# Two transformer blocks in one kernel: how the second block's gate tiles, pooling products and attention heads are joined

## The chip, the cores and the metric

The kernel runs on one core of a Trainium2 chip. The time is the device time of that core in microseconds (us), taken over several executions; the median is given. A profiled execution is one more execution, with its own time. Of the core's engines the text names TensorE (PE, matrix products), VectorE (DVE), ScalarE (ACT), GpSimd (POOL) and SyncE (SP, which here only issues DMAs).

## The reference

Everything is float32, batch 1, 512 tokens, width 2048. A first block of two layers (windowed attention, latent attention, gates) comes ahead; the change does not touch its arithmetic. The second block adds 16 meta tokens in front and computes, with `W_in` of 2048 x 12288 cut in eight:

```
h = rmsnorm_2(x, gain); zin = h @ w_in
q, k, v, g_attn, u, g_pool, m_attn, m_pool = split(zin)     # 1024 each, m_* 2048
o_attn = stick_breaking_attention(q, k, v) * silu(g_attn)   # 8 heads of 128
y_attn = o_attn @ w_attn_up
pooled = multiscale_pool(u)       # trailing means over 2, 4, 8, 16 tokens, less u
mixed  = einsum('blgc,gcd->blgd', pooled, pool_w)           # 4 groups of 256
o_pool = mixed * pool_scale * silu(g_pool)
y_pool = o_pool @ w_pool_up
merged = sigmoid(m_attn) * y_attn + sigmoid(m_pool) * y_pool
out = rmsnorm_2(x + merged @ w_out, final_gain)[:, 16:]
```

In stick-breaking attention a query takes sigmoid(z) of a key times the product of (1 - sigmoid(z)) over the keys between.

## The kernel before

**Products.** Activations lie with features on the 128 partitions and tokens along the columns. Every float32 operand is split into a high part (fp32r, cast by ACT) and a low part (difference, DVE), and a product is three matmuls (`mm3`, L167). A plain tile of 128 output features takes 2 weight blocks of 8 chunks, 48 matmuls of 512 columns; from an operand of 1024 features it takes one block and 24 matmuls. A weight block (512 KB) goes through `w_raw` (L192, SP's queue, three buffers), then `load_w_split` (L239) on ACT and DVE; `next_w` (L249) keeps two split blocks ready.

**Pairs.** Two tiles together can be made by a seven-product scheme (`run_pair`, L345): 168 matmuls of half the columns in place of 192 half-column ones. It needs sums of the activations, the eight t sets (`t_set`, L323: two POOL additions, four DVE sums, two splits each), and sums of weight blocks, which POOL's queue makes in DRAM ahead of time (`plan_sums`, `sum_step`, L204 and L218; 39 pairs, four DMAs each, paced by weight loads). The second block's pairs run with `tset`, which `t_build` (L1156) makes as a side task.

**Order.** PE's instructions run in the order in which the program writes them; the other engines' order is chosen when the kernel is built, close to the program's. `SEQ2` (L63) is the order of the second block's tiles: `gp` (silu gates of the pool, 8), then for each of four groups two `u` tiles and the pool product `pw`, then `k`, `q`, `v` (8 each), `ma`, `mp` (16 each), `ga` (8, plain), `pu` (pool-up, 16), `au` (attention-up, 16). `_plain` (L73) says which tiles are not made in pairs: `ga`, and `gp` below GPLAIN.

**Side tasks.** Beside the tiles run generators: `scales` (L879), `t_build`, eight `sb_head` (L989) and `meta_final` (L1101). `start_side` gives one a due time, `tick` (after each `mm3`) steps at most three of them whose time has come, and a `yield n` sets the next due time n later. The time is the kernel's own count: a matmul of 512 columns adds 512 / 2.4 + 3 = 216.3, in nanoseconds by intention. `need(ready)` (L307) runs the side tasks at once until a condition holds. The head with number n starts at the tile that `HEADS` (L43) gives, ahead of that tile's matmuls.

**A head** loads its q, k, v from DRAM, splits them, transposes v (`vt`), makes the scores (`zA`, `zB`, `zC`), softplus and suffix sums (`suf`, on POOL; split into `sufh`, `sufl`), the meta part (`zm`), a second phase on the same PSUM tiles (`zA<-sufl`), `rm`, then exp and the output (`so`). `meta_final` waits for all heads, and adds the meta tokens' part to each head's output (`om`), times the gate, into `oa`, which the `au` tiles read; a `need` stands ahead of the first `au` tile.

**Memory.** Working tiles come from one pool of 76 slots (`NSLOT`, L39). X2, the block's input, takes 32 of them until the last `ga` tile, the t sets 32 until the first `ga` tile, three tiles of scales stay. DMAs of the second block: `load` (L1151), the heads' loads and most stores are issued by POOL; weight loads by SP; the stores of the sigmoid gates by ACT. `o_load` (L1169) brings the eight `o_pool` tiles (`ol`) back for the pool-up tiles.

Of the kernel before, what the change touches and what calls it, by code (L numbers as in the profile page):

```python
# [18 lines left out]
P = 128  # L19
S = 512  # L20
# [17 lines left out]
GRP = 3  # L38
NSLOT = 76  # L39
M2 = NM // 2  # L40
GPLAIN = 4
EARLYT = 4
HEADS = {("ga", 0): 0, ("ga", 1): 1, ("ga", 3): 2, ("ga", 5): 3, ("ga", 6): 4, ("pu", 0): 5, ("pu", 3): 6, ("pu", 5): 7}  # L43
HN = S // 2
NPLAIN = 4
NSPILL = 8
SUMPAIRS = 39
NSIDE = 3
TP_WAIT = 4000

# [12 lines left out]
def _order2():  # L63
    seq = [("gp", i) for i in range(8)]
    for g in range(4):
        seq += [("u", 2 * g), ("u", 2 * g + 1), ("pw", g)]
    for kind, n in (("k", SB), ("q", SB), ("v", SB), ("ma", NC), ("mp", NC), ("ga", SB), ("pu", NC), ("au", NC)):
        seq += [(kind, i) for i in range(n)]
    return seq

# [33 lines left out]
def trunk_kernel(ctx, tc, xT, w_in, w_qkv, w_out, w_in2, w_pool, w_aup, w_pup, w_out2, metaT, vec, cst, outT):  # L104
# [41 lines left out]
    def split(src, name, cols=S, hi=None, lo=None):  # L146
        if hi is None:
            hi = slot(name + "h", F32R, cols)
            lo = slot(name + "l", F32R, cols)
        nc.scalar.copy(hi, src)  # L150
        tt(lo, src, f32(hi), ALU.subtract)
        return hi, lo
# [96 lines left out]
    def next_w():  # L249
        while len(wready) < 2 and wq:  # L250
            if callable(wq[0][0]):
                make, n = wq.popleft()
                load_w_split(make(), n)
            else:
                load_w_split(*load_w_dma())
            last_pe[1] += 1
            if last_pe[1] > 12 and last_pe[1] % 3 and presum:
                sum_step()
        return wready.popleft()

# [728 lines left out]
    def sb_head(hd):  # L989
        raw = {}  # L990
        for kind, n in (("k", W), ("q", S), ("v", W)):
            raw[kind] = slot(kind + "r", F32, n)
            nc.gpsimd.dma_start(raw[kind], qkvd[kind][:, hd, :])
        yield 6000
        kh, kl = split(raw["k"], "k", W)
        qh, ql = slot("qh", F32R), slot("ql", F32R)
        nc.scalar.mul(qh, raw["q"], SB_SCALE)
        stt(ql, raw["q"], SB_SCALE, f32(qh), ALU.mult, ALU.subtract)
        vf = raw["v"]
        nc.gpsimd.tensor_copy(halves(VM[:, hd * NM:(hd + 1) * NM]), halves(vf)[:, :, :M2])  # L1000
        raw = None
        yield 1500
        vh, vl = v_split(vf)
        yield 600
        zb = [ps_at("zA"), ps_at("zB"), ps_at("zC", 256)]

        def region(j, frm=None):
            frm = j if frm is None else frm
            bk, c0 = WHERE[j]
            return bk, slice(c0 + (frm - j) * P, c0 + (NB - j) * P)  # L1010

        def ks(j):
            return slice(token(j), token(j) + P)

        mm3(zb[0], kh[:, ks(0)], kl[:, ks(0)], qh, ql, True, False)
        mm(zb[0][:, :P], ident_r, maskB[:, :P], False, True)
        mm3(zb[2], kh[:, ks(2)], kl[:, ks(2)], qh[:, 256:], ql[:, 256:], True, False)
        mm(zb[2][:, :P], ident_r, maskB[:, :P], False, True)
        mm(zb[1], ident_r, maskB, True, False)
        mm3(zb[1][:, :384], kh[:, ks(1)], kl[:, ks(1)], qh[:, 128:], ql[:, 128:], False, False)  # L1020
        mm3(zb[1][:, 384:], kh[:, ks(3)], kl[:, ks(3)], qh[:, 384:], ql[:, 384:], False, True)
        spf = [softplus(z, "sp") for z in zb]
        spt = [split(t, "sp", t.shape[1]) for t in spf]

        suf = {}
        below = spf[1][:, 384:]
        for j in (2, 1, 0):
            n = (NB - j) * P
            bk, sl = region(j)
            t = slot("suf", F32, n)  # L1030
            nc.gpsimd.tensor_tensor(t[:, P:], spf[bk][:, sl][:, P:], below, ALU.add)
            nc.gpsimd.tensor_copy(t[:, :P], spf[bk][:, sl][:, :P])
            below = t
            suf[j] = split(t, "suf", n)
        suf[3] = tuple(t[:, 384:] for t in spt[1])
        yield 2500
        zo = (hd % 2) * 240 + 112
        nc.vector.tensor_copy(halves(zwh[:, zo:zo + NM]), halves(f32(kh))[:, :, :M2])
        nc.vector.tensor_copy(halves(zwl[:, zo:zo + NM]), halves(f32(kl))[:, :, :M2])
        win = slice(zo - NM * hd, zo - NM * hd + P)  # L1040
        pm = ps_at("zm")
        mm3(pm, zwh[:, win], zwl[:, win], qh, ql, True, True)
        if hd == 0:
            nc.scalar.copy(zM, pm)
        else:
            tt(zM, pm, zM, ALU.add)
        yield 6000

        def sp(j, frm=None):
            bk, sl = region(j, frm)  # L1050
            return spt[bk][0][:, sl], spt[bk][1][:, sl]

        for j in range(NB):
            bk, sl = region(j)
            mm2(zb[bk][:, sl], tri[:, :P], *sp(j), False, True)
            if j < NB - 1:
                n = (NB - 1 - j) * P
                bk, sl = region(j, j + 1)
                mm2(zb[bk][:, sl], none, suf[j + 1][0][:, :n], suf[j + 1][1][:, :n], False, True)
        yield 1000  # L1060
        pm = ps_at("rm")
        mm2(pm, nwin[:, 112 - NM * hd:240 - NM * hd], *suf[0], True, True)
        if hd == 0:
            nc.scalar.copy(RM, pm)
        else:
            tt(RM, pm, RM, ALU.add)
        At = []
        for z in zb:
            a = slot("A", F32, z.shape[1])
            act(a, z, AF.Exp)  # L1070
            At.append(split(a, "A", z.shape[1]))
        yield 7000
        o = ps_at("so")
        for j in (0, 1, 2, 3):
            bk, sl = region(j)
            vs = slice(j * P, (j + 1) * P)
            mm3(o[:, j * P:], vh[:, vs], vl[:, vs], At[bk][0][:, sl], At[bk][1][:, sl], j == 0, j == 3)
        orw = slot("oraw")
        nc.scalar.copy(orw, o)
        o_raw[hd] = orw  # L1080

    def token(j):

# [5 lines left out]
            transp(tp[:, j * P:(j + 1) * P], vf[:, token(j):token(j) + P])  # L1089
        return split(tp, "v")  # L1090

    o_raw = {}
    gates = {}
    oa = [None] * SB
    od = tc.dram_tile([P, 8, S], F32, name="od")
    gpd = tc.dram_tile([P, 8, S], F32, name="gpd")
    ypd = tc.dram_tile([P, NC, S], F32, name="ypd")
    sgd = tc.dram_tile([P, 2 * NC, S], F32, name="sgd")
    qkvd = {k: tc.dram_tile([P, SB, n], F32, name=k + "d") for k, n in (("k", W), ("q", S), ("v", W))}

    def meta_final():  # L1101
        while len(o_raw) < SB:
            yield 500
        sp = split(softplus(zM, "spm"), "spm")
        yield 4000
        pm = ps_at("lm")
        mm2(pm, tri[:, P:], *sp, True, True)
        L = slot("Lm")
        nc.gpsimd.tensor_tensor(L, zM, RM, ALU.add)
        tt(L, pm, L, ALU.add)  # L1110
        act(L, L, AF.Exp)
        Ah, Al = split(L, "Am")
        pv = ps_at("vmt", P)
        transp(pv, VM)
        vm = slot("vm", F32, P)
        nc.scalar.copy(vm, pv)
        vmh, vml = split(vm, "vm", P)
        yield 5000
        for hd in range(SB):
            mh = small.tile([P, 2 * P], F32R, tag="mh", name="mh", bufs=2)  # L1120
            nc.vector.tensor_scalar(mh[:, :P], f32(vmh), rowm[:, hd:hd + 1], None, op0=ALU.mult)
            nc.vector.tensor_scalar(mh[:, P:], f32(vml), rowm[:, hd:hd + 1], None, op0=ALU.mult)
            ps = ps_at("om")
            mm3(ps, mh[:, :P], mh[:, P:], Ah, Al, True, True)
            t = o_raw.pop(hd)
            tt(t, ps, t, ALU.add)
            tt(t, t, gates.pop(("a", hd)), ALU.mult)
            oa[hd] = split(t, f"oa{hd}")
            yield 3000

# [19 lines left out]

    def load(src, name, n=S):  # L1151
        t = slot(name, F32, n)
        nc.gpsimd.dma_start(t, src)
        return t

    def t_build(get, upto):  # L1156
        while len(tset) < upto:
            n = len(tset)
            tset.append(t_set(get(n), get(n + 8)))
            yield 5000  # L1160

    def u_order(t):

# [3 lines left out]
        return u  # L1167

    def o_load(c):  # L1169
        op[c] = split(load(od[:, c, :], "ol"), f"o{c}")  # L1170

    start_side(t_build(x2, 8))
    for kind, i in SEQ2:
        if (kind, i) in HEADS:
            if kind == "ga" and i == 0:
# [5 lines left out]
        if kind == "pw":  # L1181
            wh, wl = next_w()
            rhs = [pooled.pop(2 * i), pooled.pop(2 * i + 1)]
            for d in range(2):
# [4 lines left out]
                    mm3(ps, wh[:, sl], wl[:, sl], *rhs[k], k == 0, k == 1)  # L1189
                t = slot("mix")  # L1190
                stt(t, ps, vcol(V_PSC + 2 * i + d), gp, ALU.mult, ALU.mult)
                nc.gpsimd.dma_start(od[:, 2 * i + d, :], t)
        elif kind == "pu":
            gp = load(sgd[:, NC + i, :], "sgl")
            yp = slot("yp")
# [20 lines left out]
        elif kind == "ga":  # L1216
            if i == 0:
                tset = None
            gates["a", i] = gate_silu(run_gemm(2, 8, x2), sr, "ga")
            if i == SB - 1:  # L1220
                X2 = None
                for c in range(8):
# [216 lines left out]
```

## Time and profile before

| | us |
|---|---|
| median of 3 runs | 2771.2 |
| lowest and highest run | 2769.97, 2774.9 |
| the profiled execution | 2775.9 |
| its span, first to last instruction | 2774.1 |
| PE busy in it | 2648.2 |
| DVE busy | 1863.0 |
| ACT busy | 1318.2 |
| POOL busy | 640.4 |

The mean granted TensorE clock of the execution is 0.976 of full speed. The first gate tile of the second block starts at 1372.6 us of the span, the last pair of its input products ends at 2189.8, the pool-up tiles run from 2345 to 2486.7, the attention-up tiles follow, and the output products fill the rest. A profile line such as `pw<-pdh,wh` names what is written and read by the program's names.

### The profile page before, as it was taken

The page shows a single profiled execution, that of the slowest core. Times are in us where ns is not written, and L with a number is a line of the kernel's source. Part 1 is how long each engine was busy: PE and PEld are TensorE (multiplying, and loading weights), DVE is VectorE, ACT ScalarE, POOL GpSimd, SP SyncE. Part 2 cuts the span into 40 slices and gives each one's busy share as a digit, 9 for nine tenths or more (in the row PEclk, how much of TensorE's full clock was granted, in tenths as well). Part 3 has the DMA queues.
Part 4 walks back from the last instruction along what each step waited for, and adds up shares of the span by engine and source line. Part 5 has one row for each costly group of instructions (what it writes and reads, how often), then busy time and mean ns, then how long its engine had stood idle before and what let it go on. Part 6 is the DMA issues. An engine that isn't in the chain of part 4 may idle for free. (4 is left out here: it accounts for less than half of the span.)

```text
span 2774.1 us, 39556 instructions
## 1 busy us (share of the span) xinstructions
PE 2648.2 (95%) x15313; PEld 2314.3 (83%) x15313; DVE 1863.0 (67%) x2697; ACT 1318.2 (48%) x2170; POOL 640.4 (23%) x645
## 2 busy tenths in 40 slices
PE   8999999999999999999979789999999998899897
PEld 6888888888788888888758779999999876778697
DVE  7767667644477667665687657677777655666687
ACT  5445455522344455543345333436666666533353
POOL 4111122222111123234433210000000223324412
PEclk9999999999999999999989899999999999999999
DMA  5454544577554454567638445545555523355465
GB/s 176 121 138 121 136 120 121 165 210 204 149 132 124 128 130 125 132 167 217 186 105 245 124 127 159 158 153 158 159 161 159 176 77 107 113 157 171 124 188 182
DMA packets 129980, 416.64 MB, mean 150 GB/s; under 512 B 15344, under 2 KB 19824, under 8 KB 129792
## 3 DMA queue, kind: packets, MB, share of 16 engines
q1 hardware_dynamic: 90176, 283.15, 32.5%
q0 software_dynamic: 34864, 122.50, 18.5%
q10 hardware_dynamic: 4752, 8.46, 0.8%
q8 instruction: 120, 1.97, 0.3%
q14 instruction: 68, 0.56, 0.1%
HBM read 376.17 MB, written 119.67 MB: 179 GB/s over the span
## 5 line engine op out<-in xcount | busy, mean ns | idle before, releaser
L245 ACT CAST wh<-wr 128x1024 fp32r<-128x1024 f32 (+2 forms) x448 | 462.1, 1031 | 663.4 <-PE mm L159 349.8
L128 DVE TENSOR_TENSOR wl<-wr,wh 128x1024 fp32r<-128x1024 f32 (+2 forms) x448 | 580.0, 1298 | 237.2 <-ACT wh L245 223.1
L159 PE MATMUL mm<-hh,wh 128*128 128x512 f32 x1024 | 410.7, 401 | 7.0 <-ACT wh L245 6.8
L159 PE MATMUL mm<-hl,wh 128*128 128x512 f32 x1024 | 404.9, 395 | 2.9 <-DVE hl L131 2.9
L159 PE MATMUL mm<-hh,wl 128*128 128x512 f32 x1024 | 404.7, 395 | 2.7 <-DVE wl L128 2.7
L221 POOL DMA_DIRECT2D wsd<-in_w_in x136 | 95.7, 705 | 708.9 <-PE mm L159 502.8
L159 PEld LDWEIGHTS mm<-hh,wl 128*128 128x128 f32 x1024 | 193.3, 189 | 48.9 <-DVE wl L128 4.3
L159 PEld LDWEIGHTS mm<-hh,wh 128*128 128x128 f32 x1024 | 193.8, 189 | 42.9 <-ACT wh L245 6.8
L159 PEld LDWEIGHTS mm<-hl,wh 128*128 128x128 f32 x1024 | 193.8, 189 | 40.3 <-DVE hl L131 5.1
L245 ACT CAST wh<-ws 128x1024 fp32r<-128x1024 f32 x117 | 122.7, 1049 | 160.7 <-PE y L159 109.4
L159 PE MATMUL y<-t34h,wl 128*128 128x256 f32 (+1 forms) x624 | 176.3, 282 | 0.0
L159 PE MATMUL y<-t34l,wh 128*128 128x256 f32 (+1 forms) x624 | 175.6, 281 | 0.0
L159 PE MATMUL y<-t34h,wh 128*128 128x256 f32 (+1 forms) x624 | 175.6, 281 | 0.0
L128 DVE TENSOR_TENSOR wl<-ws,wh 128x1024 fp32r<-128x1024 f32 x117 | 143.0, 1223 | 28.5 <-ACT wh L245 26.1
L159 PE MATMUL x<-Xl,wh 128*128 128x256 f32 (+1 forms) x544 | 154.6, 284 | 0.0
L159 PE MATMUL x<-Xh,wl 128*128 128x256 f32 (+1 forms) x544 | 154.2, 284 | 0.0
L159 PE MATMUL x<-Xh,wh 128*128 128x256 f32 (+1 forms) x544 | 153.9, 283 | 0.0
L159 PEld LDWEIGHTS y<-t34h,wh 128*128 128x128 f32 x624 | 117.7, 189 | 0.0
L159 PEld LDWEIGHTS y<-t34l,wh 128*128 128x128 f32 x624 | 117.4, 188 | 0.0
L159 PEld LDWEIGHTS y<-t34h,wl 128*128 128x128 f32 x624 | 117.2, 188 | 0.0
L128 DVE TENSOR_TENSOR ws<-ws,wr 128x1024 f32<-128x1024 f32 x78 | 106.4, 1364 | 2.6
L159 PEld LDWEIGHTS x<-Xh,wh 128*128 128x128 f32 x544 | 103.4, 190 | 0.0
(1048 smaller groups left out, 7216.8 us busy)
## 6 DMA issues: line engine op xcount, KB each, us to landing
wr<-in_w_in SPq DMA_DIRECT2D x254, 512.0 KB, 3.7
wsd<-in_w_in POOLq DMA_DIRECT2D x136, 512.0 KB, 5.3
wr<-in_w_out SPq DMA_DIRECT2D x95, 512.0 KB, 4.4
ws<-wsd SPq DMA_DIRECT2D x39, 512.0 KB, 4.3
wr<-wsd SPq DMA_DIRECT2D x39, 512.0 KB, 4.1
wsd<-in_w_out POOLq DMA_DIRECT2D x20, 512.0 KB, 5.8
xd<-xn SPq DMA_DIRECT2D x32, 256.0 KB, 3.3
sgd<-sga ACTq DMA_DIRECT2D x32, 256.0 KB, 2.2
```

The lines of the kernel that those rows point to most:

```text
L128: nc.vector.tensor_tensor(out, a, b, op)
L159: last_pe[0] = nc.tensor.matmul(out, a, b, start=start, stop=stop, skip_group_check=True).ins
L221: i = nc.gpsimd.dma_start(dst, src, **kw)
L245: nc.scalar.copy(hi, raw)
```

## The change

Five things, all in the second block:

1. GPLAIN 4 to 6: gate tiles 4 and 5 are plain; one pair less, so 38 pairs of weight sums. The sums' pace goes from two in three weight loads to three in four. `t_build` starts 9000 later in the kernel's time, and leaves 7000 between sets instead of 5000 (also for the four sets that it makes in the output stage).
2. In each pooling group the two `k` tiles of the same number (one pair) stand between the `u` pair and `pw`.
3. Heads start at other tiles, and most of their yields are longer.
4. `load` and the heads' loads are issued by SP instead of POOL.
5. A head's output goes to DRAM (`od`, by ACT's queue), the attention gates go to DRAM (`gad`, by POOL's), and `meta_final` reads both back, two heads ahead (`o_gate`). The pool outputs get an array of their own (`opd`).

```diff
-GPLAIN = 4
+GPLAIN = 6
-HEADS = {("ga", 0): 0, ("ga", 1): 1, ("ga", 3): 2, ("ga", 5): 3, ("ga", 6): 4, ("pu", 0): 5, ("pu", 3): 6, ("pu", 5): 7}
+HEADS = {("ga", 0): 0, ("ga", 2): 1, ("ga", 4): 2, ("ga", 6): 3, ("pu", 1): 4, ("pu", 3): 5, ("pu", 5): 6, ("pu", 7): 7}
-SUMPAIRS = 39
+SUMPAIRS = 38
@@ _order2
-        seq += [("u", 2 * g), ("u", 2 * g + 1), ("pw", g)]
-    for kind, n in (("k", SB), ("q", SB), ("v", SB), ("ma", NC), ("mp", NC), ("ga", SB), ("pu", NC), ("au", NC)):
+        seq += [("u", 2 * g), ("u", 2 * g + 1), ("k", 2 * g), ("k", 2 * g + 1), ("pw", g)]
+    for kind, n in (("q", SB), ("v", SB), ("ma", NC), ("mp", NC), ("ga", SB), ("pu", NC), ("au", NC)):
@@ next_w
-            if last_pe[1] > 12 and last_pe[1] % 3 and presum:
+            if last_pe[1] > 12 and last_pe[1] % 4 and presum:
@@ sb_head
-            nc.gpsimd.dma_start(raw[kind], qkvd[kind][:, hd, :])
-        yield 6000
+            nc.sync.dma_start(raw[kind], qkvd[kind][:, hd, :])
+        yield 9000
...
-        yield 1500
+        yield 2000
         vh, vl = v_split(vf)
-        yield 600
+        yield 1000
...
-        yield 2500
+        yield 3500
...
-        yield 6000
+        yield 7000
...
-        o_raw[hd] = orw
+        nc.scalar.dma_start(od[:, hd, :], orw)
+        o_raw.append(hd)
@@ meta_final
+    def o_gate(hd):
+        return load(od[:, hd, :], "or"), load(gad[:, hd, :], "gar")
...
+        og = [o_gate(0), o_gate(1)]
...
-            t = o_raw.pop(hd)
+            t, g = og.pop(0)
+            if hd + 2 < SB:
+                og.append(o_gate(hd + 2))
             tt(t, ps, t, ALU.add)
-            tt(t, t, gates.pop(("a", hd)), ALU.mult)
+            tt(t, t, g, ALU.mult)
@@ load, t_build, o_load
-        nc.gpsimd.dma_start(t, src)
+        nc.sync.dma_start(t, src)
...
-            yield 5000
+            yield 7000
...
-        op[c] = split(load(od[:, c, :], "ol"), f"o{c}")
+        op[c] = split(load(opd[:, c, :], "ol"), f"o{c}")
...
-    start_side(t_build(x2, 8))
+    start_side(t_build(x2, 8), 9000)
...
-                nc.gpsimd.dma_start(od[:, 2 * i + d, :], t)
+                nc.gpsimd.dma_start(opd[:, 2 * i + d, :], t)
...
-            gates["a", i] = gate_silu(run_gemm(2, 8, x2), sr, "ga")
+            nc.gpsimd.dma_start(gad[:, i, :], gate_silu(run_gemm(2, 8, x2), sr, "ga"))
```

## Rows read from the trace of the kernel before

**Rows 1.** The page's first two parts: PE's busy time with its share of the span and its instructions, and the granted TensorE clock in forty equal slices, in tenths of full speed (9 is 0.9 or more).

```profile
PE 2648.2 (95%) x15313; PEld 2314.3 (83%) x15313; DVE 1863.0 (67%) x2697; ACT 1318.2 (48%) x2170; POOL 640.4 (23%) x645
...
PEclk9999999999999999999989899999999999999999
```

**Rows 2.** The list of PE's waits over the whole span: who waited on which tile and for whom, then us in total, how many times, and the longest.

```profile
PE pw L159 <- ACT pdh L150: 25.9, 7, 6.5
PE z L159 <- ACT t12h L150: 13.4, 3, 7.7
PE csum L159 <- ACT csh L150: 10.2, 2, 8.4
...
PE mm L159 <- DVE wl L128: 6.8, 3, 4.2
PE vt L163 <- DMA vr<-vd: 6.0, 1, 6.0
PE zA L159 <- DVE sufl L128: 5.7, 6, 1.4
PE pw L159 <- DVE pdl L128: 5.6, 4, 1.8
PE mm L159 <- ACT o0h L150: 4.7, 1, 4.7
...
PE zA L159 <- ACT qh L997: 3.2, 1, 3.2
...
PE vt L163 <- ACT RM L1064: 2.9, 1, 2.9
PE mm L159 <- ACT o1h L150: 2.3, 1, 2.3
```

**Rows 3.** The table of stretches. Each stretch begins and ends at the first matmul of a piece on PE's timeline (those of the pool products begin where the pair before has ended); its width in us, then the busy time of PE, its weight loads, DVE, ACT and POOL with counts, the granted clock, the busy share of the DMA engines and GB/s.

```profile
1372.60:1396.38 23.78, 15.27 (x56) 11.64 (x54) 19.23 (x26) 8.97 (x17) 10.75 (x7) 0.78 0.35 95
1396.38:1407.59 11.21, 11.21 (x50) 9.01 (x49) 9.15 (x12) 4.03 (x8) 6.33 (x6) 1.00 0.50 140
1430.01:1469.40 39.39, 23.96 (x169) 22.46 (x168) 32.40 (x40) 18.71 (x27) 16.20 (x15) 0.78 0.52 133
1469.40:1489.27 19.87, 19.87 (x170) 19.87 (x169) 16.43 (x19) 12.46 (x18) 8.13 (x9) 1.00 0.91 302
1489.27:1509.75 20.48, 20.48 (x170) 20.44 (x168) 15.30 (x19) 11.61 (x18) 8.57 (x9) 1.00 0.94 272
1509.75:1520.12 10.37, 5.62 (x14) 3.30 (x13) 7.67 (x9) 3.04 (x6) 3.07 (x4) 0.67 0.70 183
...
1610.40:1628.38 17.98, 6.48 (x15) 3.90 (x14) 7.48 (x9) 3.08 (x6) 11.19 (x11) 0.62 0.20 62
1628.38:2189.80 561.42, 561.42 (x4706) 561.42 (x4704) 420.88 (x504) 291.55 (x375) 17.95 (x32) 1.00 0.52 159
2189.80:2344.99 155.19, 138.38 (x636) 112.91 (x635) 91.43 (x131) 101.18 (x183) 48.62 (x62) 0.96 0.30 92
2344.99:2486.70 141.71, 128.95 (x562) 104.17 (x563) 88.15 (x140) 65.26 (x113) 44.64 (x71) 0.93 0.45 143
2486.70:2632.19 145.49, 136.76 (x577) 109.15 (x576) 96.74 (x111) 45.69 (x61) 67.83 (x67) 0.98 0.48 152
```

**Rows 4.** POOL's timeline in the gate stretch and at the last pooling group: start, duration, instruction, and in brackets the idle time before it and what ended it.

```profile
1414.91 1.38 POOL L439 TENSOR_TENSOR gpg<-gpg,gpa 128x512 f32<-128x512 f32 x1 [9.27 <-ACT gpa L135]
...
1417.22 1.34 POOL L330 TENSOR_TENSOR ra<-Xh,Xl 128x528 f32<-128x528 f32 x1
...
1617.74 1.25 POOL L1138 TENSOR_TENSOR pl<-uf 128x527 f32<-128x527 f32 x1 [2.13 <-ACT uf L1166]
```

**Rows 5.** DVE's timeline, the same columns, in the gate stretch, at the last pooling group and late in the attention-up tiles.

```profile
1381.39 1.54 DVE L128 TENSOR_TENSOR t<-ra,rb 128x264 f32<-128x264 f32 x1
...
1388.18 0.43 DVE L128 TENSOR_TENSOR t<-ra,rb 128x264 f32<-128x264 f32 x1
...
1390.89 0.68 DVE L128 TENSOR_TENSOR csl<-xgq,csh 128x512 fp32r<-128x512 f32 x1
...
1622.64 0.69 DVE L131 SCALAR_TENSOR_TENSOR pd<-pl,uf 128x512 f32<-128x512 f32 x1 [4.57 <-POOL pl L1138]
1624.07 0.69 DVE L128 TENSOR_TENSOR pdl<-pd,pdh 128x512 fp32r<-128x512 f32 x1 [0.74 <-ACT pdh L150]
...
2582.85 0.69 DVE L128 TENSOR_TENSOR ym<-mm,sgl 128x512 f32<-128x512 f32 x1 [2.89 <-DMA sgl<-sgd]
```

**Rows 6.** POOL's timeline, the same columns, at the start of the pool-up tiles and at the start of the last head.

```profile
2344.52 1.26 POOL L439 TENSOR_TENSOR gag<-gag,gaa 128x512 f32<-128x512 f32 x1 [9.89 <-ACT gaa L135]
2345.73 3.76 POOL L1153 DMA_DIRECT2D ol<-od  x7
...
2404.48 0.55 POOL L1197 DMA_DIRECT2D ypd<-yp  x1 [2.08 <-DVE yp L128]
2405.01 0.54 POOL L993 DMA_DIRECT2D kr<-kd  x1
```

**Rows 7.** The view of the tile om: durations in ns (lowest, median, highest), the first and the last start in us, and the shape. Each of the eight steps has two of these matmuls.

```profile
L159 PE MATMUL om<-Amh,mh x16: 392/395/468, 2450.4 to 2475.3; 128*128 128x512 f32 x16
```

**Rows 8.** The list of DMA issues: transfer, queue, count, size of each, and the median us from issue to landing.

```profile
ol<-od POOLq DMA_DIRECT2D x8, 256.0 KB, 4.6
```

**Rows 9.** The list of waits of SP's queue from 2180 to 2600 us, with the columns of rows 2.

```profile
SPq L193 <- DVE wl L128: 371.6, 52, 23.1
```

More of the change, by code (lines that the diff above doesn't have):

```diff
@@ L1090, in v_split @@
         return split(tp, "v")
-    o_raw = {}
-    gates = {}
+    o_raw = []
     oa = [None] * SB
     od = tc.dram_tile([P, 8, S], F32, name="od")
+    opd = tc.dram_tile([P, 8, S], F32, name="opd")
+    gad = tc.dram_tile([P, SB, S], F32, name="gad")
     gpd = tc.dram_tile([P, 8, S], F32, name="gpd")
@@ L1218, in trunk_kernel @@
                 tset = None
-            gates["a", i] = gate_silu(run_gemm(2, 8, x2), sr, "ga")
+            if i >= SB - 2:
+                pass
+            nc.gpsimd.dma_start(gad[:, i, :], gate_silu(run_gemm(2, 8, x2), sr, "ga"))
             if i == SB - 1:
```

## The prediction

> **What bounds the kernel now.** I read the page first [rows 1]: TensorE (PE) is busy for 2648 of 2774.1 us, 95%, and no other engine passes 67%. So the time is PE's work, plus what PE waits, plus what it runs at the lower of its two clocks. The digits of the granted clock drop below 9 in only two of forty slices, so the losses lie in a few places; the list of PE's waits [rows 2] names them: pooled tiles ahead of their product (pdh, pdl: 31.5 us), the t sets ahead of the first pair (t12h: 13.4), the column sum in the first gate tile (csh: 10.2, of which 8.4 in one piece), then operands of heads (vr, RM, sufl, qh), of the pool-up tiles (o0h, o1h) and a weight split at the last joint (wl).
>
> The third view is the table of stretches [rows 3]. Their ends are the first matmuls of each piece on PE's timeline. It prices the work where nothing disturbs it: a plain gate tile (48 matmuls of 512 columns) takes 11.21 us, a gate pair 19.87, a pair of u, k or v 20.48. Against these the reader sees what each joint costs: the first gate tile 23.78 instead of 11.21, the first gate pair 39.39 instead of 19.87, and a pool product with its wait 10.37 in the first group and 17.98 in the last, at a granted clock of 0.67 and 0.62. That is a mix of 1.2 and 2.4 GHz: the clock fell after PE had idled, so the matmuls behind a wait are slow as well. The 28 pairs from 1628 to 2190 run with PE busy throughout at clock 1.00; nothing is to be had there. The profiled execution took 2775.9 us, 4.7 above the median; the sum below is made against 2775.9 and then carried to the median.
>
> **Gate stretch (1372.6 to 1489.27, 116.67 us).** Two gate tiles leave the pair form. Work after: 6 x 11.21 + 19.87 = 87.1, against 4 x 11.21 + 2 x 19.87 = 84.6 before, so plain tiles cost 2.5 more; the six small column-sum matmuls add some 1.5 to either. What is won is two waits.
> The first: t_build starts with no delay and its first two sets are issued ahead of the second part of scales(). On VectorE (DVE) the second set's four sums stand before csl [rows 5], and PE waits 8.4 us. With the delay of 9000 all of scales() (steps at 0, 6000 and 7500 of the kernel's clock) is issued before the first set. I take this wait at 0; at worst it stays.
> The second: the sets are late although their steps end at 35,000 of the 41,500 that four tiles take. Two causes show. GpSimd (POOL) stands 9.3 us ahead of a gate's last product and the next set's ra sits behind it [rows 4], and DVE stretches: a sum that takes 0.43 alone took 1.54 while POOL worked [rows 5]. After the change the steps fall at 9 + 7n thousand, the last at 58,000 of 62,300, so 1.6 sets a tile rather than 2.2, and DVE has no pair's splits among them. The last set can be held behind the fifth gate's product on POOL: that tile ends at 5 x 11.2 = 56 us from the stretch's start, the product came 4.2 us after the last ga tile's end (2344.52 on POOL [rows 6]; PE stopped 4.7 before 2344.99 [rows 2, 3]), then 1.3 for it, 0.6 for its store, 2.7 for ra and rb and some 3 for sums and splits, 68; PE needs that set at 67.2 + 1.5 + 2.5 = 71. It is met with 3 us to spare. I leave 3 us for what I don't see (bounds 0 and 12). Term: 116.7 - 87.1 - 1.5 - 3 = **-25** (-28 to -16).
>
> **Pooling (1489.27 to 1628.38, 139.1 us).** A pool product is 12 matmuls, 2.8 us at the plain tile's rate. In the last group the second tile's pdl ends at 1624.76 [rows 5], 14.4 us after its u pair; a k pair of 20.48 now stands between, which covers it with 6 us over. Work: 4 x 20.48 + 4 x 2.8 = 93.1, so 46 us are open. Against full cover: POOL's 20 additions of about 1.3 us [rows 4] now run beside a k pair's splits on DVE, which needs 15.3 of a pair's 20.5 us [rows 3]; DVE also stands up to 4.57 us before pd [rows 5], and PE has two split weights of 2.93 us in hand. In slots, X2 (32), the t sets (32) and three scales hold 67 of 76; pooled tiles and a k pair want 8 more. I leave 4 us (0 to 11). Term **-42** (-46 to -35). The moved k pairs cost the same where they go; their stores stay on POOL. pw's gpl now waits in SP's queue; that queue runs about three weights ahead, so the load is early.
>
> **Heads (2189.80 to 2486.70, 296.9 us).** The two rows [rows 3] give 16.8 + 12.8 = 29.6 us of PE idle, and clocks of 0.96 and 0.93, worth 6.2 + 9.9 = 16 us (partly the same time). Where they go [rows 2]: vt 8.9 (vr and RM; head 7's loads stood behind a ypd store that waited for DVE [rows 6]), sufl 5.7, qh 3.2, the first pool-up tile 7.0 (o0h, o1h; seven ol loads stood behind the last gate's product [rows 6]). After: loads go by SP, where no product stands before them, and 9000 instead of 6000 is left before the split; POOL's order can't hold them. vt falls to 0.5, qh to 0. From z to the second phase 10,500 instead of 8,500 is left, and the waits were at most 1.4 each, so sufl goes to 1. For ol the ends are 0 and 7.0; the split still stands behind the last gate on DVE, so I keep 3. Idle falls by 20, and of the clock's 16 I take 10 with it. New costs: heads 4 to 7 start two pool-up tiles apart, and head 7 two tiles later. From its start 30,500 to its end and 33,000 of meta_final follow, while nine tiles of 5,190 and the steps' own matmuls are some 61,000: about two of eight om steps fall to the need() ahead of the attention-up tiles. An om step came every 3.5 us [rows 7], so 0 to 8 us; I take 4. The DRAM trips of od and gad are read two heads ahead, and an ol load of the same size lands in 4.6 us [rows 8]: nothing, while two om steps take longer than that. Term **-26** (-36 to -12).
>
> **Attention-up and first out tiles (2486.70 to 2632.19).** PE idles 8.7 us [rows 3]: late ym steps of DVE wait up to 2.9 us for sgl [rows 5], a load that stands behind the ym product of the tile before in POOL's queue; then four t sets, five units apart, hold wl for 4.2 [rows 2]. On SP the loads don't wait for POOL, and seven units apart the sets leave room. Term **-7** (-10 to +3, if the loads hold weights in SP's queue instead).
>
> At nothing: one sum pair less and the faster pace (PE never waits for wsd in [rows 2]; DMA is at half its share in most stretches of [rows 3]; if it did bind, the price would be a landing, 4.6 us [rows 8]). The out stage is unchanged. SP's 104 added issues fall into its waits for wl, 371 us in this part alone [rows 9].
>
> Sum: -25 - 42 - 26 - 7 = -100; 2775.9 - 100 = 2676, and from the median 2771.2 - 100 = **2671**.
>
> **A rule that speaks against it.** The ol rows [rows 6] show loads delayed by what stands before them on POOL, and the terms go by that. The Trainium skill, page DMA: Bandwidth & Descriptors, section Issuing engines are not separate DMA queues, says that DMAs from any engine share the same DMA engines, and that another issuer saves the issue time alone. By it the queue move gives next to nothing; that is the second rival.
> POOL's additions and DVE's splits stretch each other in the rows above. The Trainium skill, page SBUF — State Buffer, section SBUF: two separate sides, says that GpSimd and a DVE operation with two SBUF inputs exclude each other for a whole instruction. The k pair brings just such splits beside the pooling; that is the fourth rival.
>
> **Rivals.**
> 1. Crowded heads. The pool-up phase holds four heads instead of three, two tiles apart. DVE goes from 62% of it to about 75%, as the last three heads with their tiles read 88 of 142 us [rows 3]. If each of the four waits what head 7 did (6.0 idle and about as much at half clock, some 9), the heads' term is 0: 2697. For: the two heads that started closest did wait. Against: head 7's wait was a load's. Chance 0.14.
> 2. The queue move saves only issue time. Then vt 8.4, qh 3.2, ol 4.0, the clock's part of them 8 and the last joint's 7 stay: 2671 + 31 = 2702. Chance 0.08.
> 3. All covered: every term at its low end, -120, 2651. Chance 0.09.
> 4. The pooling moves rather than hides. The 14 additions of groups 3 and 4, and of them those that meet a split, cost DVE up to 8 us beyond the pair's 5 us of room, and PE loses it twice, waiting and at half clock, with pd's wait: +20, 2691. Chance 0.09.
> 5. Slower. A load in SP's queue that waits for a slot holds all weights behind it; POOL's loads never did. In the pooling stretch only nine slots are free, and eight gpl loads pass there. SP's longest wait now is 23.1 us [rows 9]; PE has three weights, 8.8 us, in hand. If every gpl stood that long, 8 x 14.3 = 114 us, 2785. It turns to a loss from 12.5 us lost per load. Against: the slots are released by DVE and POOL steps of a few us. Chance 0.06, 0.02 of it near no change.
>
> **How the numbers follow.** My forecast holds 0.54, its own range 2655 to 2690. From rivals 1, 2 and 4 the range must reach to about 2706, from rival 3 down to 2646; outside are most of rival 5 and tails of 0.1. About 0.2% can be told from no change here, 5.5 us: all but rival 5 are faster by more. Faster 0.94, same 0.02, slower 0.04.
>
> **What would show it.** The wait list without pdh and pdl, and the clock at 1.00 from the first u pair on, confirm the largest term; pw waits of over 3 us each refute it. The first gate tile should take 12 to 14 us, the only gate pair 20 to 23. In the heads' stretch vt and o0h should be gone, and a wait at the first oa tile should be new. A wait for wl in the pooling stretch speaks for rival 4, SP waiting for a slot for rival 5. The prediction fails if the k pair's own operands are late, since the largest term hangs on that cover.

## The result, and the profile after

The changed kernel took 2726.9 us (median of 4 runs, 2723.6 to 2731.0), the kernel before beside it 2773.1: a ratio of 0.983 (95% interval 0.981 to 0.986). The forecast was 2671, with a range of 2646 to 2706. The change is faster, as forecast, but by 46 us and not by 100. The profiled execution took 2724.0 us, 51.9 less than the one of before, and the table splits these 51.9 us; its last column is the kernel of the ninth experiment below.

| stretch (first matmul to first matmul), us | before | forecast | after | change | ninth run |
|---|---|---|---|---|---|
| up to the first gate tile | 1372.6 | 0 | 1370.3 | -2.3 | 1371.3 |
| gate tiles | 116.7 | -25 | 101.2 | -15.5 | 92.2 |
| u pairs, pool products, k pairs | 221.0 | -42 | 195.6 | -25.4 | 175.7 |
| the other input pairs | 479.5 | 0 | 478.2 | -1.3 | 478.8 |
| heads: ga and pool-up tiles | 296.9 | -26 | 281.1 | -15.8 | 269.5 |
| attention-up and first out tiles | 145.5 | -7 | 148.0 | +2.5 | 134.4 |
| out stage to the end | 141.9 | 0 | 147.8 | +5.9 | 144.9 |

(For before, the third row is the pooling's 139.1 and four k pairs of 20.48, and the fourth is without these.) Each column is one execution. Over the kernels below that leave a stretch as the change made it, the gate tiles took 100.2 to 102.6 us, the heads 280.5 to 283.1, the attention-up tiles 145.3 to 148.0 and the out stage 147.4 to 150.6, and the first gate tile began between 1369.8 and 1373.9. So a difference of 2 or 3 us in one row says nothing: the attention-up tiles gained nothing rather than lost 2.5. The after column is the table of stretches of the changed kernel, with the columns of [rows 3]:

```profile
1370.28:1471.47 101.19, 91.96 (x463) 76.58 (x462) 93.12 (x108) 51.20 (x78) 38.47 (x30) 0.97 0.32 103
1471.47:1667.07 195.60, 181.17 (x1395) 178.19 (x1393) 139.93 (x167) 78.75 (x107) 40.12 (x39) 0.96 0.48 144
1667.07:2145.29 478.22, 478.22 (x4033) 478.22 (x4032) 363.65 (x437) 260.00 (x339) 14.06 (x27) 1.00 0.53 162
2145.29:2426.39 281.10, 257.39 (x1197) 210.46 (x1196) 172.71 (x268) 166.57 (x296) 67.34 (x91) 0.96 0.47 154
2426.39:2574.36 147.97, 139.92 (x578) 112.45 (x577) 85.16 (x111) 43.32 (x57) 46.31 (x33) 0.95 0.45 144
2574.36:2722.20 147.84, 127.88 (x1045) 125.42 (x1043) 113.88 (x148) 68.76 (x90) 31.26 (x30) 0.95 0.55 179
```

PE was still idle for 14.4 us of the second stretch, 23.7 of the heads and 8.1 of the attention-up tiles, and the granted clock was 0.95 to 0.97 in every stretch in which it idled. The list of PE's waits over the whole span answers to [rows 2]:

```profile
PE x L159 <- ACT m L364: 15.9, 4, 8.4
PE mm L159 <- DVE wl L128: 11.5, 6, 4.9
PE vt L163 <- DMA vr<-vd: 9.5, 2, 5.8
PE mm L159 <- DVE ym L128: 8.0, 2, 5.4
PE mm L159 <- ACT o0h L150: 7.0, 1, 7.0
```

The names: x, y and z are the accumulators of a pair's products and m a copy of one of them, ym is an attention-up tile times its gate, sgl and ypl are the gate and the pool-up tile that are loaded for it.

The waits for pdh, pdl, t12h, sufl and qh are gone, csh's is down from 10.2 to under 1. In their place x waits for a copy m, which is new, and plain tiles wait 11.5 us for wl and 8.0 for ym, where it was 6.8 and 3.4 before. vt waits 9.5 us for vr, against 6.0 for vr and 2.9 for RM before; o0h waits 7.0, as o0h and o1h did together. Each of the five was read to its cause in the trace; the experiments test these readings.

**x waits for m.** ScalarE's (ACT) timeline in the last pooling group (start, duration, instruction, idle time before it):

```profile
1647.80 0.62 ACT L150 CAST pdh<-pd 128x512 fp32r<-128x512 f32 x1 [6.52 <-issue]
1648.32 1.04 ACT L245 CAST wh<-ws 128x1024 fp32r<-128x1024 f32 x1
1649.27 0.37 ACT L362 COPY m<-z 128x264 f32<-128x264 f32 x1
1649.54 0.38 ACT L364 COPY m<-x 128x264 f32<-128x264 f32 x1
```

and what the cast stood for, on DVE:

```profile
1647.03 0.69 DVE L131 SCALAR_TENSOR_TENSOR pd<-pl,uf 128x512 f32<-128x512 f32 x1 [2.29 <-POOL pl L1146]
```

ACT idles 6.5 us ahead of the second tile's pdh, which needs pd, which needs POOL's last addition. The k pair's products z and x are long done, but their copies m stand behind that cast, and PE's next product adds into x, so it may only start when x has been copied: it starts at 1649.97, after 8.4 us of waiting. PE then runs that product at a granted clock of 0.50, the lower level, 5.45 us for 2.9. Three of the four waits are in the pooling stretch, 14.3 us; the fourth, 1.5 us, is at the first pair of the out stage.

**Plain tiles wait for wl.** DVE, and POOL at the same time, in the fourth gate tile, and DVE's next such split, in the sixth:

```profile
1410.59 6.67 DVE L128 TENSOR_TENSOR wl<-wr,wh 128x1024 fp32r<-128x1024 f32 x1
1417.18 0.42 DVE L128 TENSOR_TENSOR t<-ra 128x264 f32<-128x264 f32 x1
...
1435.73 6.56 DVE L128 TENSOR_TENSOR wl<-wr,wh 128x1024 fp32r<-128x1024 f32 x1
```

```profile
1408.71 1.38 POOL L439 TENSOR_TENSOR gpg<-gpg,gpa 128x512 f32<-128x512 f32 x1 [4.69 <-ACT gpa L135]
...
1411.00 1.34 POOL L330 TENSOR_TENSOR ra<-Xh,Xl 128x528 f32<-128x528 f32 x1
1412.29 1.33 POOL L331 TENSOR_TENSOR rb<-Xh,Xl 128x528 f32<-128x528 f32 x1
1413.58 1.31 POOL L330 TENSOR_TENSOR ra<-Xh,Xl 128x528 f32<-128x528 f32 x1
1414.86 1.31 POOL L331 TENSOR_TENSOR rb<-Xh,Xl 128x528 f32<-128x528 f32 x1
```

A weight split of 1.2 us took 6.7, and ended 1.1 us after POOL's fourth sum. The planner had spaced the sets; POOL, which waits for each gate's product, ran two of them in a row. The first long split cost PE only 0.4 us. The second, also beside four POOL sums, cost 4.9; between them a set's split that took 3.56 us in place of 0.7 made the next weight split late by 2.7. These are the 8.1 us of the 11.5 that fall in the gate tiles.

**vr, o0h and ym wait.** SP's queue where head 0 loads; its ga tile began at 2145.29:

```profile
2158.80 0.33 SPq L193 DMA_DIRECT2D wr<-in_w_in  x1
2159.18 0.42 SPq L993 DMA_DIRECT2D kr<-kd  x1
2159.70 0.38 SPq L993 DMA_DIRECT2D qr<-qd  x1
2160.17 0.38 SPq L993 DMA_DIRECT2D vr<-vd  x1
```

The loads go out right behind the next weight load, which waits until DVE's split frees a raw buffer. Head 0's are so issued 13.9 us after its tile began; the ol loads stood behind a weight load at 2274.12, and the late sgl loads of the attention-up tiles behind one at 2521.35.

### The profile page after: what moved, and what is told of

Its sections match the earlier page's. It is cut to its first block, busy times and chain, and to the rows that moved or that the text cites. A ratio compares the mean times of both kernels' runs of the same rounds, so it can differ in the third digit from the quotient of the medians.

```text
span 2722.2 us, 39422 instructions
## 1 busy us (share of the span) xinstructions
PE 2632.6 (97%) x15241; PEld 2304.9 (85%) x15241; DVE 1839.9 (68%) x2686; ACT 1312.7 (48%) x2165; POOL 590.4 (22%) x561
## 5 line engine op out<-in xcount | busy, mean ns | idle before, releaser
L159 PE MATMUL x<-Xh,wh 128*128 128x256 f32 (+1 forms) x528 | 151.6, 287 | 14.8 <-ACT m L364 14.3
L159 PEld LDWEIGHTS x<-Xh,wl 128*128 128x128 f32 x528 | 101.6, 192 | 1.0 <-DVE wl L128 1.0
```

The source lines that it names most:

```text
L159: last_pe[0] = nc.tensor.matmul(out, a, b, start=start, stop=stop, skip_group_check=True).ins
```

## The experiments

Each kernel is the changed one with the edit shown. Medians stand beside runs of the kernel before on the same chip, with their ratio; the changed kernel's is 0.983.

**1. The pooled tile's last step late.**

```
         cur = t
         n *= 2
+    yield 14000          # issued as a side step from here
     d = slot("pd")
     stt(d, cur[:, NM:], 1.0 / w, uf[:, NM:], ...)
-    return split(d, "pd")
+    pooled[j] = split(d, "pd")
 ...
 if kind == "pw":
+    need(both tiles of the group)
```

> The changed kernel with one edit: a pooled tile's last step (pd and its split) is issued 14,000 of the planner's units behind the additions, so behind the k pair's copies m on ScalarE's queue, and no longer ahead of them. Theory (ScalarE's order): in the changed kernel the cast pdh waits for pd, pd for POOL's last addition, and the copy m of the k pair stands behind that cast; so the wait of x for m (15.9 us in 4, the longest 8.4) goes to under 1 us, the stretch from the first u pair to the first q pair falls from 195.6 to 177 to 182, and the total falls by 14 to 19 us. Rival (the pooling itself is too slow beside the pair's splits): the wait only moves to the pooled product, pw then waits for pdh or pdl by as much as x did, and the stretch stays over 190.

2706.9 us, ratio 0.973 (0.969 to 0.977). The stretch, and the only wait left in it:

```profile
1474.10:1649.68 175.58, 174.95 (x1395) 172.65 (x1393) 143.53 (x167) 79.55 (x107) 46.34 (x38) 1.00 0.51 160
```

```profile
PE y L160 <- DVE ab L129: 0.6, 1, 0.6
```

It gained 20.0 us, at clock 1.00: a little more than the theory gave, and the wait did not move to pw. (The theory put all four waits here; the fourth, at the out stage, stays at 1.5 us.) ACT's order was the cause; POOL's additions and the pair's splits then go side by side at a loss of 0.6 us to PE.

**2. The sets' sums ra and rb on VectorE, gate stretch only.**

```
-    nc.gpsimd.tensor_tensor(ra, ...); nc.gpsimd.tensor_tensor(rb, ...)
+    nc.vector.tensor_tensor(ra, ...); nc.vector.tensor_tensor(rb, ...)
```

> The changed kernel with one edit: the two sums ra and rb of each of the first eight t sets run on VectorE and not on POOL. Theory (POOL's sums stretch VectorE's): beside ra and rb the weight split took 6.67 and 6.56 us, alone 1.21; without them every split of the gate stretch takes 1.2 to 1.5 us, the waits of mm for wl (11.5 us in 6) fall under 3, and the stretch from the first gate tile to the first u pair falls from 101.2 to 91 to 95, 6 to 10 us in all. Rival (VectorE simply has too much to do in that stretch, 93 of 101 us): 16 sums of about 0.7 us more on it, 11 us, make it as late or later: 101 to 110 us, with the waits for wl as long as now.

2716.4 us, ratio 0.977 (0.973 to 0.980). DVE at the same place, and the stretch:

```profile
1412.25 0.70 DVE L331 TENSOR_TENSOR rb<-Xh,Xl 128x528 f32<-128x528 f32 x1
...
1413.90 1.21 DVE L128 TENSOR_TENSOR wl<-wr,wh 128x1024 fp32r<-128x1024 f32 x1
```

```profile
1371.41:1463.62 92.21, 90.29 (x463) 76.54 (x462) 82.64 (x124) 51.68 (x78) 20.22 (x14) 0.98 0.35 112
```

DVE has 16 operations more (124 for 108) and is busy 10.5 us less. No wait for wl is left in it; the 5.0 us that the whole span still has, against the theory's 3, lie elsewhere. The stretch gained 9.0 us; POOL's sums were the cause, and the rival, that DVE has too much to do, is out.

**3. Head loads through POOL.**

```
-    nc.sync.dma_start(raw[kind], qkvd[kind][:, hd, :])
+    nc.gpsimd.dma_start(raw[kind], qkvd[kind][:, hd, :])
```

> The changed kernel with one edit: the three loads of each head (k, q, v) are issued by POOL again, 9000 units ahead of their split, while all other loads stay on SP. Theory (SP's order): a head's loads stand on SP behind a weight load that waits for a free raw buffer, so head 0's were issued 14 us after its tile began; on POOL they go out within 9 us of it, the waits of vt for vr (9.5 us in 2) fall under 2, and the stretch from the first ga tile to the first attention-up tile falls from 281.1 to 272 to 277. Rival (which queue issues a load changes only its own issue time): the loads land as late as before, within 1 us, and vt waits 8 to 10 us. A third way: POOL's gate product holds the loads instead, then the waits move to other heads, and the sum of the waits for qh, kh and vr stays at 6 to 12.

2730.3 us, ratio 0.982 (0.978 to 0.986); the stretch took 283.8 us, no shorter than 281.1. Head 0's loads went out at 2148.2, 0.6 us after its tile began, and its wait of 5.8 us is gone. But the last two heads waited 4.3 and 4.8. POOL at the last one shows why:

```profile
2354.75 0.55 POOL L993 DMA_DIRECT2D kr<-kd  x1
2357.08 0.54 POOL L1205 DMA_DIRECT2D ypd<-yp  x1 [1.78 <-DVE yp L128]
2357.65 0.54 POOL L993 DMA_DIRECT2D qr<-qd  x1
2358.18 0.54 POOL L993 DMA_DIRECT2D vr<-vd  x1
```

A ypd store that waits for DVE holds its q and v; at the head before, all three loads stood behind such a store. The third way came in its number, 9.1 us in all, though a store and not a gate product is what held the loads: each queue has a place where something waits. That the issuer makes no difference is refuted at head 0.

**4. sgl and ypl one tile earlier.**

```
-    ga, yp = load(sgd[:, i, :], "sgl"), load(ypd[:, i, :], "ypl")
+    if i + 1 < NC:
+        ahead.append(gate_in(i + 1))
+    ga, yp = ahead.pop(0)
```

> The changed kernel with one edit: the two loads sgl and ypl of an attention-up tile are issued on SP one tile earlier. Theory (SP's order): in the changed kernel they stand behind weight loads that wait for a raw buffer, landed up to 4.5 us after PE had done the tile, and PE waited 8.0 us for the buffers that ym frees; one tile earlier these waits go under 1.5 us, and the stretch from the first attention-up tile to the first out pair falls from 148.0 to 136 to 141; the first out pair, whose weights were late, may win up to 6 more. Rival (the t sets crowd VectorE there): the waits for ym stay, or return as waits for wl, and the stretch stays at 145 or more.

2718.9 us, ratio 0.978 (0.974 to 0.982). The waits for ym are gone, but the stretch stayed at 147.5: the theory's cause was real and its gain was taken by the rival's. The new waits, 2.0 us of wl at an attention-up tile, the rest at the fourth weight block of the out tiles (three of which are made together, so this is the second half of the first):

```profile
PE mm L159 <- DVE wl L128: 6.2, 2, 4.2
PE mm L159 <- ACT wh L245: 2.2, 1, 2.2
```

POOL runs eight sums in a row from 2527.68 there, and DVE beside it:

```profile
2530.65 1.48 POOL L330 TENSOR_TENSOR ra<-mg5h,mg5l 128x512 f32<-128x512 f32 x1
2532.08 1.47 POOL L331 TENSOR_TENSOR rb<-mg13h,mg13l 128x512 f32<-128x512 f32 x1
```

```profile
2530.89 1.52 DVE L128 TENSOR_TENSOR t<-ra,rb 128x256 f32<-128x256 f32 x1
...
2540.22 0.41 DVE L128 TENSOR_TENSOR t<-ra 128x256 f32<-128x256 f32 x1
```

The out stage fell from 147.8 to 141.2: its first pair found its weights and copies ready, since PE reached it later.

**5. Run 4, and all sets of the out pairs summed on VectorE.** The edit is that of run 2 at the other calls of t_set.

> The kernel of the run before (sgl and ypl one tile earlier) with one edit more: all ra and rb of the out pairs' t sets run on VectorE. In that run the late loads were gone, but the waits came back as two waits for a weight (6.4 us at the second out tile), while POOL made eight sums in a row and VectorE's operations beside them took 1.5 us in place of 0.42. Theory (POOL's sums stretch VectorE's): without them the waits for wl and wh after the attention-up tiles fall under 2 us, the stretch from the first attention-up tile to the first out pair falls from 147.5 to 136 to 140, and the total is 14 to 20 us below the changed kernel's 2726.9. Rival (order alone: four whole sets stand on VectorE ahead of a weight's split, and 16 sums more make it longer): waits of 5 us or more stay, and the stretch stays over 144.

2708.5 us, ratio 0.976 (0.974 to 0.979). The two stretches:

```profile
2427.38:2562.21 134.83, 134.83 (x577) 109.27 (x576) 95.73 (x129) 45.28 (x61) 26.21 (x19) 0.99 0.49 158
2562.21:2707.65 145.44, 126.03 (x1045) 124.21 (x1043) 112.03 (x146) 66.50 (x88) 29.91 (x29) 0.96 0.56 181
```

The first is 134.8, better than expected and 12.6 below run 4, with PE busy all through it. The out stage is at 145.4, which gives 4.2 of these back: its first pair waits 1.7 us for m, as in the changed kernel (1.5), and a later tile for wh by 1.7. The trace has m at 2571.99 on ACT behind the last plain out tile's square, which had waited for DVE:

```profile
2570.70 0.63 ACT L135 ACTIVATE oq<-hs 128x512 f32<-128x512 f32 x1 [2.95 <-DVE hs L128]
```

That is run 1's cause at another joint; no run took it away here.

**6. Heads 0 to 3 through POOL, 4 to 7 through SP one tile earlier.**

```
-    nc.sync.dma_start(raw[kind], ...)
+    (nc.gpsimd if hd < 4 else nc.sync).dma_start(raw[kind], ...)
-    yield 9000
+    yield 9000 if hd < 4 else 14200
-    ("pu", 1): 4, ("pu", 3): 5, ("pu", 5): 6, ("pu", 7): 7
+    ("pu", 0): 4, ("pu", 2): 5, ("pu", 4): 6, ("pu", 6): 7
```

> The changed kernel with one edit: heads 0 to 3 load through POOL, whose loads for them went out within 5 us of the tile's start in the run with all heads on POOL; heads 4 to 7 load through SP, but start one pool-up tile earlier and wait 14,200 units in place of 9000 before their split. Theory (each load stands behind an instruction in its own queue that waits: SP's behind the next weight load, POOL's behind a ypd store): with neither ahead of it, no head waits for its load, the waits of vt fall from 9.5 us to under 1.5, and the stretch from the first ga tile to the first attention-up tile falls from 281.1 to 268 to 275. Rival (the heads are crowded, so that a wait taken from one comes back at another): the waits for rm, so, zC and the om steps grow by as much, and the stretch stays at 278 or more.

2714.5 us, ratio 0.978 (0.975 to 0.980). The stretch is 272.9, 8.3 less; no wait for a head's load is left. Its largest waits:

```profile
PE mm L159 <- ACT o0h L150: 6.8, 1, 6.8
PE zA L159 <- DVE vl L128: 2.6, 2, 2.3
PE rm L159 <- ACT A L135: 2.4, 2, 1.9
```

The two lower ones are new, crowding of about 5 us; the theory holds with a part of the rival in it.

**7. The ol loads ahead of the last ga tile.**

```
+    if i == SB - 1:
+        early = [load(opd[:, c, :], "ol") for c in range(8)]
 ...
+        op[c] = split(early[c] ...)      # behind the tile, as before
```

> The changed kernel with one edit: the eight ol loads of the pool-up tiles are issued ahead of the last ga tile and not behind it (they need no slot of X2 then). Theory (SP's order and the landing): o0h waited 7.0 us because the loads stood behind a weight load and landed 6.3 us after the tile's end; issued earlier, only the cast and the split are left, so the wait is 0.5 to 2.5 us and the stretch from the first ga tile to the first attention-up tile falls by 4 to 8 from 281.1. Rival (the splits stand behind the last gate on VectorE and ScalarE anyway): the wait stays at 4 us or more. The loads may also wait for slots and hold the last ga tile's weights: then a wait for wl or wh of several us shows in that tile.

2726.4 us, ratio 0.982 (0.980 to 0.985); the stretch stayed at 281.2. o0h's wait fell only to 4.6, while a wait for sufh of 0.9 came ahead of it. The rival is right for most of it: the loads were there, and the cast stood on ACT behind the last gate's first step:

```profile
2279.81 0.63 ACT L135 ACTIVATE gaa<-gag 128x512 f32<-128x512 f32 x1 [1.73 <-DVE gag L128]
2280.34 0.60 ACT L150 CAST o0h<-ol 128x512 fp32r<-128x512 f32 x1
```

**8. Run 2 with four plain tiles.**

```
-GPLAIN = 6
+GPLAIN = 4
-SUMPAIRS = 38
+SUMPAIRS = 39
 ...
-    yield 7000
+    yield 4500 if eng is nc.vector else 7000
```

> The kernel with ra and rb of the first eight sets on VectorE, with one edit more: four plain gate tiles as in the kernel before (two gate pairs), the sets 4500 units apart. It asks whether the two tiles taken out of the pair form were needed. Theory (POOL's sums were what made the sets late, the two tiles bought time for nothing else): work is 84.6 us by the kernel before's rows, the first pair waits under 4 us, and the stretch from the first gate tile to the first u pair is 86 to 91, against 92.2 with six plain tiles. Rival (eight sets are more than VectorE can do beside four tiles): the first pair waits for t12h or t12l by 6 us or more and the stretch is 95 or more.

2732.8 us, ratio 0.985 (0.983 to 0.987). The stretch (1372.54 to 1479.23) took 106.7 us, 14.5 more than run 2:

```profile
PE z L159 <- ACT t12h L150: 13.4, 4, 4.3
PE z L159 <- DVE t12l L128: 2.2, 4, 1.1
```

The theory falls, for the rival's reason: DVE is busy for 40.4 of the 45.0 us of the four plain tiles, so with all sums on it an earlier start could win 4.6 at most, of 15.6 us of waits. With POOL's sums out of the way, the two tiles taken out of the pair form are still needed.

**9. The edits together.** Those of runs 1, 2, 5 and 6, and that of run 7 with the splits of the first two ol tiles made inside the last ga tile.

> The changed kernel with the edits that gave something, together: the pooled tile's last step late, all t sets' sums on VectorE, sgl and ypl one tile earlier, heads 0 to 3 through POOL and 4 to 7 one tile earlier on SP; and with the ol loads ahead of the last ga tile also the splits of the first two of them inside that tile, since in the run with the loads alone the cast o0h still stood behind the last gate's steps on ScalarE. Theory (five separate waits, each in its own stretch): the single gains by stretch add up, 20.0 for the pooling, 9.0 for the gate tiles, 13.1 and 2.4 for the attention-up and out tiles, 8.3 for the heads, and 4 to 7 more for o0h: 2666 to 2674. Rival (they share VectorE and slots, so a gain of one is paid in the next stretch): over 2685.

2667.9 us (5 runs, 2665.4 to 2669.2), ratio 0.961 (0.959 to 0.963). The gains add up, and the last column of the first table has them by stretch. From the gate tiles on no single wait of PE is over 4 us; the largest left there is for the third ol tile, the first whose split was not made early, so the joint of run 7 gave 3.4 us and not 4 to 7:

```profile
PE mm L160 <- ACT o2h L151: 3.9, 1, 3.9
```

**10. Run 9 with the k pairs behind the pooling.**

```
-    ..., ("u", 2 * g + 1), ("k", 2 * g), ("k", 2 * g + 1), ("pw", g)
+    ..., ("u", 2 * g + 1), ("pw", g)      # k pairs after the groups
```

> The kernel with all edits together, with the k pairs moved back behind the pooling as in the kernel before: it prices the reorder of the change alone, once the cast pdh no longer stands ahead of the k pair's copies. Theory (the k pair hides the pooled tile's whole chain, some 14 us in the last group): without it the four products wait again by 25 to 40 us in all, and with the half clock behind them the stretch of the eight u pairs, eight k pairs and four products is 40 to 50 us longer. Rival (with the late step the pooling would have been covered without the k pair, by two split weights in hand): 0 to 15 us longer.

2713.0 us, ratio 0.978 (0.976 to 0.980).

```profile
1463.49:1602.09 138.60, 107.75 (x723) 97.54 (x722) 88.79 (x99) 48.38 (x72) 38.45 (x31) 0.84 0.38 119
1602.09:2163.05 560.96, 560.96 (x4706) 560.96 (x4705) 420.91 (x504) 291.47 (x375) 18.49 (x34) 1.00 0.51 159
```

```profile
PE pw L160 <- ACT pdh L151: 30.5, 6, 8.3
```

Up to the first ga tile that is 699.6 us against run 9's 654.5: the reorder is worth 45.0 us, 30.7 of it waits and the rest the clock (0.84 in that stretch).

## Why the prediction was off, step by step

No one term makes up the miss. Pooling is off by 17 us, the gate tiles, the heads and the attention-up tiles by 9 to 10 each, the out stage by 6. The heads and the attention-up tiles came inside their own bounds, near the bad end, and the gate tiles just outside; pooling came 10 us beyond its bound, and the out stage was put at nothing.

**Pooling, -42 forecast, -25.4 measured: the step that failed.** That "a k pair of 20.48 now stands between, which covers it" was right on length: with the cast late the reorder gives 45 us (runs 1 and 10), almost all of the 46 that were open. What failed is that the cover was checked by time alone. The prediction looked at DVE's room, POOL's additions and slots, and not at ACT's order, where the waiting cast stood ahead of the cover's own copies; none of the five rivals had it either. Run 1 prices it at 20.0 us: PE idles 13.8 less, and the work itself takes 6.2 less at the higher clock. The warning at the end spoke of the k pair's own operands and had no price; late were the copies of its products. The sign set for this term came by half: pdh and pdl left the wait list, but the clock of the stretch was 0.96 and not 1.00.

**Gate tiles, -25 forecast, -15.5 measured: a term of the wrong size.** csl's wait went, as forecast, and run 8 shows the two plain tiles to be needed. "I leave 3 us for what I don't see" should have been 12.6 (101.2 less the work of 87.1 and 1.5), just past its bound of 12. [Rows 5] already had a sum that took 1.54 beside POOL's work in place of 0.43, and [rows 4] POOL standing 9 us ahead of a product: the steps were taken as evenly spaced on POOL because the planner spaces them, and the stretched splits weren't counted. (Its 1.6 and 2.2 sets a tile divide 11.2 measured us by the planner's units; in these a tile is 10,382, and they are 1.5 and 2.1.) Run 2 took 9.0 of the 12.6 back.

**Heads, -26 forecast, -15.8 measured.** sufl and qh went as forecast. The step "loads go by SP, where no product stands before them" failed: no product, but weight loads that wait. vr and o0h wait 9.5 and 7.0, where 0.5 and 3 were forecast. The om steps left over cost 4.3 us of waits for mh, as priced (4).

**Attention-up and out tiles, -7 and 0 forecast, +2.5 and +5.9 measured.** In the changed kernel PE waited in the first of these for ym alone, 8.0 us, as SP's order made sgl late (run 4). POOL's eight sums, which hold DVE, cost PE waits only once that was gone; run 5 took them away, and both edits together gave 13.1. Seven units between the sets left no room, because POOL reached all four only behind the last ym product. "The out stage is unchanged" left out its first pair, which waited 3.6 us in the changed kernel and 0.5 before: 2.1 for a weight's cast and splits and 1.5 for the copy m, both behind the plain tiles' last steps. This is read from the trace and not shown by a run.

**The rivals.** Rival 2 has the waits about right, but for qh's, which is gone, and the mechanism wrong: by it the loads would have come no earlier from another queue, but head 0's went out 13.3 us earlier after its tile's start on POOL than on SP (0.6 against 13.9, run 3), and its wait vanished. The rule beside it, in the Trainium skill, page DMA: Bandwidth & Descriptors, section Issuing engines are not separate DMA queues, says that another issuer saves only the time of the issue. For a transfer that has been issued no run here contradicts it, but at head 0 the issue itself came 13.3 us earlier: these runs paid for what stood ahead of it. Rival 4's mechanism is there, but in the wrong stretch: in the pooling run 1 left PE 0.6 us of waits, while in the gate tiles POOL's sums cost 9.0 us (run 2) and at the out tiles 12.6 (run 5 against run 4), of which 4.2 came back in the out stage. The page SBUF — State Buffer of the Trainium skill, section SBUF: two separate sides, says that GpSimd and a DVE operation with two SBUF inputs exclude each other for a whole instruction; the split that ended 1.1 us after POOL's fourth sum, and takes 1.2 alone, agrees. Rivals 1, 3 and 5 didn't come: no wait of the changed kernel is a crowded head's of over 1 us, and no weight was late in the pooling stretch. The step that rival 5 feared is there, though: four of the gpl loads stood in SP's queue until a kd store had landed and its slot was free, 20.5 us in all and 5.8 at most, which is less than the 8.8 us of weights that the prediction reckoned PE to have in hand.

**What stays open.** The last cause named for the out stage, 4 us in runs 5 and 9; how much of run 6's 8.3 us is POOL's heads and how much the earlier start; and what the new pace of the weight sums and the DRAM trips of od and gad are worth, which no run takes back.

## What to carry to other kernels

Work put between a slow chain and its user hides it only if no in-order queue has a waiting instruction of the chain ahead of the cover's own steps: walk each engine's order, and issue the chain's last step as late as its user allows. A load moved to another queue trades what stands ahead of it there, so look for the instruction that waits (here a weight load, a product, a store) before moving it. Before spacing steps on a planner's clock, check that the engine which runs them isn't itself released in bursts.

## What the runs showed of the hardware

One weight split on DVE stood through four POOL sums in a row, 6.67 us for 1.21, while shorter DVE sums went one for one with POOL's, 1.52 beside 1.48 at the out tiles (run 4). POOL lost little in the gate tiles (1.31 to 1.34 a sum) and more at the out tiles (1.45 to 1.75, where its first sum took 1.28). In run 2 two more operations per set on DVE made DVE 10.5 us less busy over the gate tiles: work given to POOL had cost DVE more than it took off it.
